# One-hots of a product-key expert layer: two tokens innermost, one compare instruction, chunks in pairs

## The chip, the cores and the metric

The kernel runs on one core of one Trainium2 chip. The metric is the device time of one execution in microseconds. TensorE (PE) multiplies matrices, VectorE (DVE) and ScalarE (ACT) do elementwise work, GpSimd (POOL) does next to nothing here, and SyncE (SP) issues the loads of weights. Every engine takes its own instructions in order.

## What is computed

The reference is a transformer of two blocks on 256 tokens of 1024 features in float32: two mixer layers with their feed-forwards, then attention, cross attention, and last a layer of 16,384 experts (PEER), which is the only part that the change touches:

```python
q = (xc @ w_q).reshape(PEER_TOK_CHUNK, PEER_HEADS, 2, half)
s = jnp.einsum("thpd,hpnd->thpn", q, subkeys)
s1, i1 = lax.top_k(s[:, :, 0], 16); s2, i2 = lax.top_k(s[:, :, 1], 16)
...                                   # the 16 best of the 16 x 16 sums, for each of 8 heads
e = jnp.take_along_axis(cand_i, top_pos, axis=-1)      # expert = 128 * i + j
g = jax.nn.softmax(top_s, axis=-1)
a = jax.nn.gelu(jnp.einsum("td,thkd->thk", xc, w_down[e]))
return jnp.einsum("thk,thkd->td", g * a, w_up[e])
```

So each token has 128 chosen experts (8 heads of 16), each with a weight g.

## The kernel before

The kernel doesn't gather. It multiplies all tokens with all 16,384 rows of `w_down`, keeps gelu of that in `act` [128 experts j, 128 chunks i, 256 tokens], multiplies it with a dense map of the weights g, which is zero for the experts that were not chosen, and multiplies the product with all of `w_up`.

**Chunks.** A chunk is 128 experts. `chunk` (line 1784) calls `lin_b`: `load` (line 223) fetches 512 KB of `pd`, ACT (L233) and DVE (L234) split it into a high and a low part (`wh`, `wl`, three buffers each), PE runs 24 matmuls of 256 columns (L257, L258, L260), and ACT takes the gelu out of PSUM. 70 chunks are done earlier, beside the routing. The other 58, the late chunks, are done between the groups of tokens described next.

**Weights of the chosen experts.** For each token the map [j, i] is a product of two one-hot matrices over the 128 slots: onehot(j) as the stationary operand, onehot(i) times g as the moving one. `iT` holds i, j and g of every slot with the slots on the partitions, `ib` holds them in float16 with g cut into a high part, and the low part stays in `iT`. A `group` (line 1849) does four tokens. Its `front` writes `oh` [128 slots, 4 kinds, 128, 4 tokens] in float16, with the four tokens innermost: DVE compares a table `rb` (0 to 127, each four times) with i, then with j (two instructions at L1854), and multiplies the first one-hot with the high part of g (L1855); ACT multiplies it with the low part, token by token (four at L1857). Its `back` runs two matmuls of 128 columns for each token (eight at L1865) into `pg`, DVE multiplies the activations of the chunks done so far with it in place (L1867), and ACT copies the rest of the map into the places of the chunks to come (L1869).

**Late chunks.** After each `back`, `upto` says how many chunks should be done by then, and `chunk(t0)` runs the missing ones. The tokens before t0 already have their weights in the chunk's place, so their gelu goes into a tile `ta` (L1792, three buffers), and DVE multiplies it in (L1796); the tokens from t0 on get their gelu directly (L1794). In the profile this is one late chunk for nearly every group.

**Order.** `pipe` runs the front of a group before the back of the group ahead of it. The tile framework then orders the instructions of each engine by priority and by its own estimates when it builds the program. `oh` has three buffers, `pg` four banks of PSUM. After the last group `lin_k` (line 341) multiplies `act` with `w_up` on PE, chunk by chunk, up to the end; `begin` starts its first three chunks a little earlier for the first 128 tokens.

Of the kernel before, what the change touches and what calls it, by code (L numbers as in the profile page):

```python
# [8 lines left out]
F32 = mybir.dt.float32  # L9
# [10 lines left out]
T = 256  # L20
# [5 lines left out]
# ---------------------------------------------------------------- host layout  # L26
# [4 lines left out]
def _pick(w, idx):  # L31
    """Columns idx of w; -1 stands for a column of zeros."""
    idx = np.asarray(idx)
    out = np.zeros((w.shape[0], len(idx)), w.dtype)
    ok = idx >= 0
    out[:, ok] = w[:, idx[ok]]
    return out


def _units(w, nk, ncol):  # L40
    """[K, N] -> units [n, 128, nk, ncol], k parts innermost among the units of a column block."""
    K, N = w.shape
    a = w.reshape(K // (128 * nk), nk, 128, N // ncol, ncol)
    return np.ascontiguousarray(a.transpose(3, 0, 2, 1, 4).reshape(-1, 128, nk, ncol))
# [6 lines left out]
def _pv(i):  # L51
    """Vectors that lie along the partitions: name -> [128, n]."""
# [28 lines left out]
def pack(i):  # L81
# [15 lines left out]
    # layer 0  # L97
# [20 lines left out]
    # layer 1  # L118
# [24 lines left out]
    # second block  # L143
# [17 lines left out]
    # constants of the shapes  # L161
# [24 lines left out]
# ---------------------------------------------------------------- kernel  # L186
def tile_kernel(tc, A, out, tap=None, stop=None):
# [7 lines left out]
    with contextlib.ExitStack() as ctx:  # L195
# [12 lines left out]
        def accs():  # L208
            """[token block][column half], tokens on partitions."""
            return [[f([128, 512], name="acc") for _ in range(2)] for f in (ps_lo, ps_at)]  # L210

        # ------------------------------------------------ helpers
# [5 lines left out]
        def pinned(*more, pins=True):  # L218
            """work of no hurry: after the instructions of the chain before it."""
            st = contextlib.ExitStack()  # L220
            for i in list(more) or (pools.pins if pins else []):
                st.enter_context(tc.issue_after(i))
            return st
# [17 lines left out]
        def ahead(*srcs):  # L241
            """fetch the weights of the next linears before what comes in between."""
# [11 lines left out]
        def mm3s(ps, pairs, start, stop):  # L254
            """the sum of mm3 over pairs (l, r), the products with the low part of r last."""
# [9 lines left out]
        def lin_b(src, u0, n, h, nk, kper, cper, evac, bank=None):  # L265
            """out^T chunks of 128 columns: units [128, kper, 128*cper], n units of columns."""
# [13 lines left out]
        def lin_n(src, h, evac):  # L280
            """as lin_b for one unit, in float32 passes without a split: where the vector engine holds the time."""
# [7 lines left out]
        def lin_a(src, u0, h, nk, kper, N, evac, between=None):  # L289
            """out [tok, N]: stationary h, moving the weights."""  # L290
# [13 lines left out]
        def split(dst, src, i=None):  # L304
            """dst pair (high, low) parts of src."""
# [13 lines left out]
        def mm_t(acc, a, w, tb, half, start, stop):  # L319
            """acc[tb][half] += a^T w: a [128, T], w [128, 2, 512]."""  # L320
# [7 lines left out]
        def tail(acc, parts, post, between=None):  # L328
            """the last parts (a, w), one token block after the other; post(acc, tb) when a block is complete;
            between: work before the second block's turn."""  # L330
# [12 lines left out]
        def lin_k(src, pool, chunks, post, turn, pre, keep=3, begun=None):  # L343
            """sum over chunks a of a^T W[k], tokens on partitions; post and turn: see tail.
            begun: the accumulators and the (a, w) of the first chunks, done for the first token block."""
# [20 lines left out]
        # ------------------------------------------------ constants  # L366
# [19 lines left out]
        # causal bias, [off block | diagonal block]  # L386
# [4 lines left out]
        def rms_steps(groups, n, out, eng=None):  # L391
            """1/rms over the features of each group of chunks, on all partitions: PSUM tiles [128, T] in out.
            groups: lists of (AP [128, w], w = T or 2T). Work for other engines fits between the steps."""
# [31 lines left out]
        def rsqrt(r, ss, scale):  # L425
            """r[:, 1] = (ss * scale + EPS) ** -0.5, r: [128, 4, ...] workspace."""
# [13 lines left out]
        def norm(src, out, n=1024, pin=False, between=None, eng=None):  # L440
            """out: [128, 1] = 1/rms of the rows of src, a list of APs [128, w]."""
# [29 lines left out]
        def rows(cols):  # L471
            """the vector cols [128, 8] along the free axis, on all partitions."""
# [10 lines left out]
        def postnorm(y, gr, tb, n, t):  # L483
            """x += gr * rmsnorm(y) for a token block, y: two PSUM halves; n: the next norm; t: [128, 2, 2, 512] workspace."""
# [26 lines left out]
        class raw:  # L511
            """the features of rmsnorm(x) * gain + shift before the division by the norm: pair h [128, 8, W],
            with the shift in columns T and T + 1 (an even number of them); r: 1/norm on all partitions, tok: with tokens on partitions."""
# [9 lines left out]
            def turn(self, tb, src=None, more=None):  # L523
                """a token block to features on partitions; more: (t, d), with diag(d) t to add to it."""
# [39 lines left out]
            def fin(self, pool, dst, ps, func=AF.Identity, scale=1.0):  # L564
                """dst = func(scale * (the linear of the normed features))."""
# [7 lines left out]
        # ------------------------------------------------ adaLN  # L573
# [24 lines left out]
        # ------------------------------------------------ attention of one head  # L598
        def pipe(jobs, lag=1):
            """jobs: (front, back) pairs; each back comes lag fronts after its own."""  # L600
# [10 lines left out]
        def attend(ap, q, k, v, o, bias, gate=None, full=False, first=True, last=True, rest=None):  # L611
            """q, k: [K, T]; v: two APs [128, dv]; o(): PSUM AP [dv, T], accumulated into unless first;
            gate: row factors [128, 2]. Returns the two parts of the work."""
# [47 lines left out]
        def after(job, f):  # L661
            """job with f() at its end."""
# [7 lines left out]
        class lazy:  # L670
            """a tile allocated at its first use."""
# [8 lines left out]
        # ================================================ layer 0 mixer  # L680
        def layer0():
            with contextlib.ExitStack() as ctx0:
# [25 lines left out]
                # the shift on the tensor engine, as a row  # L708
# [55 lines left out]
                def conv(c, ps):  # L764
                    """chunk c of the channels xs | B | C."""
# [20 lines left out]
                # dt and dt * a, tokens on partitions  # L786
# [23 lines left out]
                # strict lower (t > s) and upper (t <= l) masks, [t, .]  # L810
# [6 lines left out]
                # rope tables of the positions (cos | sin with the signs), the same on every 32 rows  # L817
# [28 lines left out]
                # S^T masked, [s, (blk0: l 0..255 | blk1: l 128..255)]  # L846
# [9 lines left out]
                # normed low rank parts of q and of k, v  # L856
# [12 lines left out]
                # xs * dt with tokens on partitions  # L869
# [167 lines left out]
        # ================================================ SwiGLU  # L1037
# [3 lines left out]
        def ffn(l):  # L1041
            with tpool(name=f"ffn{l}", bufs=2) as F:
# [56 lines left out]
                # keys and values of the memory, in the time of the norms  # L1099
# [35 lines left out]
        # ================================================ layer 1 mixer  # L1135
        def layer1():
            with contextlib.ExitStack() as ctx1:
# [22 lines left out]
                # ---- gated linear attention: cumulated log decay, [dk, t]  # L1160
# [15 lines left out]
                # gates with tokens on partitions: [128, qb, (head, branch)]  # L1176
# [21 lines left out]
                def evt(dst):  # L1198
                    """to tokens on partitions."""
# [11 lines left out]
                # ---- constants  # L1211
                # level masks [s, t]: t >= s and t xor s >= 2 ** level
                with pinned():
# [15 lines left out]
                    # bias of the heads: -slope * (q - k), masked; [off block | diagonal block]  # L1229
# [9 lines left out]
                    # the same for the compressed keys  # L1239
# [15 lines left out]
                # compressed keys and values  # L1255
# [3 lines left out]
                # [high | low] parts of the keys or values  # L1259
# [58 lines left out]
                def scores():  # L1318
                    """compressed scores: [128 q, qb, head, 32]"""
# [28 lines left out]
                # A^T [s, (head, blk0: t 0..255 | blk1: t 128..255)], level by level  # L1348
# [57 lines left out]
                def gla(hh):  # L1406
                    """with tokens on partitions."""
# [80 lines left out]
        # ================================================ MoBA + gMLP  # L1488
        def mix2():
            with contextlib.ExitStack() as ctx2:  # L1490
# [7 lines left out]
                # perm[k, m] = 1 where k = m ^ 32  # L1498
# [61 lines left out]
                # gMLP  # L1560
# [52 lines left out]
        class add_t:  # L1613
            """x += a^T W, units of 2 chunks and half of the columns; n: the next norm."""
# [5 lines left out]
            def go(self, tb, u):  # L1620
                """unit u for a token block."""
# [9 lines left out]
            def run(self, n, pre, first, last, post=None):  # L1631
                """first, last: units for both blocks together, for one after the other."""
# [16 lines left out]
        # ================================================ memory cross attention  # L1649
# [35 lines left out]
        # ================================================ PEER  # L1685
        def peer():
            with contextlib.ExitStack() as ctx4:
# [51 lines left out]
                def route(hh):  # L1739
                    """in steps, for other work in between; the last ones decode the chosen."""  # L1740
# [43 lines left out]
                def chunk(t0):  # L1784
                    """activations of 128 experts; the weights of the tokens before t0 stand in their place."""
# [3 lines left out]
                    def evac(_, ps):  # L1789
                        if t0:  # L1790
                            t = W4.tile([128, T], F32, name="ta", tag="ta", bufs=3)
                            S.activation(t[:, :t0], ps[:, :t0], AF.Gelu_apprx_tanh)  # L1792
                        if t0 < T:
                            S.activation(act[:, c, t0:], ps[:, t0:], AF.Gelu_apprx_tanh)  # L1794
                        if t0:
                            V.tensor_tensor(act[:, c, :t0], act[:, c, :t0], t[:, :t0], op=ALU.mult)  # L1796
# [14 lines left out]
                # softmax of the chosen scores (the first is the largest)  # L1811
# [20 lines left out]
                # 2 ** 15 times the weights in two parts of 11 bits and a sign: what a float32 holds  # L1832
                flat = sel.rearrange("p a b c -> p (a b c)").bitcast(F16)
                ib = flat[:, :1024].rearrange("p (e t) -> p e t", e=4)
                rb = flat[:, 1024:].rearrange("p (i t) -> p i t", t=4)
# [125 lines left out]
```

## Time and profile before

| | us |
|---|---|
| median of the timed runs | 1946.98 (1945.98 to 1949.31, 3 runs) |
| span of the profiled execution | 1948.3 |
| PE busy in it | 1911.8 (98%) |
| DVE busy | 1522.7 (78%) |
| ACT busy | 1129.0 (58%) |
| mean granted clock of TensorE | 0.993 |

Matmuls overlap in their pipeline, so a busy PE in the profile may still have room; how fast they follow one another is read from their starts. The stage that the change touches runs from 1357 to 1582 us, between the routing and the product with `w_up`.

### The profile page before, as it was taken

Reading aid. Unit: us, or ns where it says so; the run is one execution under the profiler, and the core shown is the slowest. Engines: PE = TensorE matmul, PEld = TensorE weight load, DVE = VectorE, ACT = ScalarE, POOL = GpSimd, SP = SyncE. Lnnn points to the kernel's source line nnn. Section 1 sums busy time; section 2 is a strip of 40 time slices with the busy share of each in tenths; the row PEclk is TensorE's granted clock in tenths of the full one; section 3 lists DMA queues with packets and bytes.
Section 4 is the critical chain, followed back from the end, with each engine's and each line's share of the span. In section 5 each row is a group of like instructions: output and inputs, shape, how many; then the busy total and the mean of one; then the engine's idle time right before and its main releaser. Section 6 shows DMA issues by size and latency. Waiting matters only on the chain.

```text
span 1948.3 us, 34549 instructions
## 1 busy us (share of the span) xinstructions
PE 1911.8 (98%) x12874; PEld 1714.4 (88%) x12874; DVE 1522.7 (78%) x3356; ACT 1129.0 (58%) x2170; POOL 12.9 (1%) x18
## 2 busy tenths in 40 slices
PE   7999999999999999999999999999999999999998
PEld 4988899999878899999988899999999988888886
DVE  7978889898778787677667798898899975555555
ACT  6876655467556555454655544445888854444444
POOL 0000000000000000000000000000000000000000
PEclk9999999999899999999999999999999999999999
DMA  9664698856316485545524455555444355555553
GB/s 331 220 205 151 203 325 276 278 193 206 122 66 229 163 312 181 176 152 178 184 92 147 133 179 180 195 181 174 149 135 141 131 185 192 186 189 190 184 191 133
DMA packets 102554, 362.12 MB, mean 186 GB/s; under 512 B 11617, under 2 KB 14689, under 8 KB 102130
## 3 DMA queue, kind: packets, MB, share of 16 engines
q1 hardware_dynamic: 100368, 357.61, 54.9%
q10 hardware_dynamic: 2018, 2.31, 0.4%
q8 instruction: 101, 1.65, 0.3%
q14 instruction: 67, 0.55, 0.1%
HBM read 357.25 MB, written 2.62 MB: 185 GB/s over the span
## 4 chain that ended last, share of the span: by engine, by line
PE 87%; DVE 7%; ACT 2%; DMA 1%; issue 1%; ACTq 0%; DVEq 0%
PE mm L257 11%; PE mm L260 11%; PE mm L258 11%; PE acc L252 10%; PE acc L250 10%; PE acc L251 10%; PE lo L257 3%; PE lo L260 3%; PE lo L258 3%; PE pg L1865 2%; DVE wl L234 2%; DVE act L1867 1%; PE sc L628 1%; PE pA L1354 1%; PE mm L250 1%
## 5 line engine op out<-in xcount | busy, mean ns | idle before, releaser
L234 DVE TENSOR_TENSOR wl<-w,wh 128x1024 fp32r<-128x1024 f32 (+1 forms) x571 | 694.7, 1220 | 159.7 <-ACT wh L233 154.2
L233 ACT ACTIVATE wh<-w 128x1024 fp32r<-128x1024 f32 (+1 forms) x571 | 598.5, 1054 | 244.3 <-PE mm L260 105.8
L257 PE MATMUL mm<-hh,wh 128*128 128x256 f32 (+1 forms) x2072 | 517.7, 287 | 4.5 <-DVE eb L569 1.4
L258 PE MATMUL mm<-hh,wl 128*128 128x256 f32 (+1 forms) x2072 | 511.9, 284 | 1.8 <-DVE wl L234 1.8
L257 PEld LDWEIGHTS mm<-hh,wh 128*128 128x128 f32 x2072 | 393.7, 190 | 9.5 <-issue 3.2
L258 PEld LDWEIGHTS mm<-hh,wl 128*128 128x128 f32 x2072 | 393.8, 190 | 4.7 <-DVE wl L234 2.5
L250 PE MATMUL acc<-wh,ah 128*128 128x512 f32 x784 | 310.7, 397 | 1.2 <-ACT ah L306 1.2
L252 PE MATMUL acc<-wh,al 128*128 128x512 f32 x784 | 309.4, 395 | 0.9 <-DVE al L307 0.9
L251 PE MATMUL acc<-wl,ah 128*128 128x512 f32 x784 | 309.6, 395 | 0.0
L260 PE MATMUL mm<-hl,wh 128*128 128x256 f32 (+1 forms) x2072 | 297.0, 283 | 0.0
L260 PEld LDWEIGHTS mm<-hl,wh 128*128 128x128 f32 x2072 | 267.9, 189 | 2.5 <-issue 2.0
L252 PEld LDWEIGHTS acc<-wh,al 128*128 128x128 f32 x784 | 147.4, 188 | 36.6 <-DVE al L307 1.3
L250 PEld LDWEIGHTS acc<-wh,ah 128*128 128x128 f32 x784 | 147.2, 188 | 35.6 <-ACT ah L306 2.2
L251 PEld LDWEIGHTS acc<-wl,ah 128*128 128x128 f32 x784 | 147.2, 188 | 33.9 <-DVE wl L234 0.3
L306 ACT ACTIVATE ah<-act 128x256 fp32r<-128x256 f32 (+1 forms) x131 | 53.7, 413 | 181.9 <-PE acc L251 177.5
L257 PE MATMUL lo<-hh,wh 128*128 128x256 f32 x520 | 128.7, 287 | 0.0
L258 PE MATMUL lo<-hh,wl 128*128 128x256 f32 x520 | 125.0, 279 | 0.0
L307 DVE TENSOR_TENSOR al<-act,ah 128x256 fp32r<-128x256 f32 (+1 forms) x131 | 54.4, 418 | 79.5 <-ACT ah L306 79.5
L586 DVE SCALAR_TENSOR_TENSOR wa<-wa,cbc 128x1024 f32<-128x1024 f32 x88 | 107.1, 1229 | 3.4 <-DMA wa<-in_ada 3.3
L1857 ACT ACTIVATE oh<-oh,iT 128x128 f16<-128x128 f16 x256 | 96.7, 572 | 4.7 <-DVE oh L1854 1.6
L257 PEld LDWEIGHTS lo<-hh,wh 128*128 128x128 f32 x520 | 98.2, 189 | 0.1
L258 PEld LDWEIGHTS lo<-hh,wl 128*128 128x128 f32 x520 | 97.9, 188 | 0.0
(567 smaller groups left out, 2448.0 us busy)
## 6 DMA issues: line engine op xcount, KB each, us to landing
w<-in_pd SPq DMA_DIRECT2D x128, 512.0 KB, 3.3
w<-in_pu SPq DMA_DIRECT2D x128, 512.0 KB, 3.2
wa<-in_ada SPq DMA_DIRECT2D x88, 512.0 KB, 4.5
w<-in_wf SPq DMA_DIRECT2D x88, 512.0 KB, 4.4
w<-in_w SPq DMA_DIRECT2D x79, 512.0 KB, 4.2
w<-in_wd SPq DMA_DIRECT2D x44, 512.0 KB, 4.1
w<-in_wo SPq DMA_DIRECT2D x32, 512.0 KB, 3.4
w<-in_pq SPq DMA_DIRECT2D x16, 512.0 KB, 3.7
```

The costliest lines, as they stand in the source:

```text
L233: S.activation(wh[:, :n], w[:, :n], AF.Copy)
L234: V.tensor_tensor(wl[:, :n], w[:, :n], wh[:, :n], op=ALU.subtract)
L250: PE.matmul(ps, lh[0], rh[0], start=start, stop=False, skip_group_check=True)
L251: PE.matmul(ps, lh[0], rh[1], start=False, stop=False, skip_group_check=True)
L252: PE.matmul(ps, lh[1], rh[0], start=False, stop=stop, skip_group_check=True)
L257: PE.matmul(ps, lh[0], rh[0], start=start and i == 0, stop=False, skip_group_check=True)
L258: PE.matmul(ps, lh[1], rh[0], start=False, stop=False, skip_group_check=True)
L260: PE.matmul(ps, lh[0], rh[1], start=False, stop=stop and i == len(pairs) - 1, skip_group_check=True)
L306: S.activation(dst[0], src, AF.Copy)
L307: return V.tensor_tensor(dst[1], src, dst[0], op=ALU.subtract).ins
L586: V.scalar_tensor_tensor(w, w, 1.0, pools.cbc, op0=ALU.mult, op1=ALU.mult, accum_out=mod[l][:, j:j + 1])
L1857: S.activation(oh[:, 3, :, t], oh[:, 0, :, t], AF.Copy, scale=iT[:, 2, t0 + t:t0 + t + 1])
```

## The change

`oh` becomes [128 slots, 4 kinds, 2 pairs of tokens, 128, 2 tokens]: two tokens are innermost, so the elements of one token's one-hot lie 4 bytes apart, where they lay 8 apart. `rb` holds each number twice, and `ib` is stored group by group, so that one instruction compares both i and j for all four tokens (1,024 elements for each slot) in the place of two of 512. The multiplication with the high part of g, the four of ACT and the eight matmuls stay, on the new layout. `upto` counts in twos, and late chunks come in pairs: two in a row after every second group or so. Their gelus go into the two halves of one tile `ta` (one buffer), and one instruction multiplies both in after the second.

```diff
-                def chunk(t0):
+                def chunk(t0, ta=None, last=True):
...
                         if t0:
-                            t = W4.tile([128, T], F32, name="ta", tag="ta", bufs=3)
-                            S.activation(t[:, :t0], ps[:, :t0], AF.Gelu_apprx_tanh)
+                            S.activation(ta[:, 1 if last else 0, :t0], ps[:, :t0], AF.Gelu_apprx_tanh)
                         if t0 < T:
                             S.activation(act[:, c, t0:], ps[:, t0:], AF.Gelu_apprx_tanh)
-                        if t0:
-                            V.tensor_tensor(act[:, c, :t0], act[:, c, :t0], t[:, :t0], op=ALU.mult)
+                        if t0 and last:
+                            V.tensor_tensor(act[:, c - 1:c + 1, :t0], act[:, c - 1:c + 1, :t0], ta[:, :, :t0],
+                                            op=ALU.mult)
...
-                ib = flat[:, :1024].rearrange("p (e t) -> p e t", e=4)
-                rb = flat[:, 1024:].rearrange("p (i t) -> p i t", t=4)
-                V.tensor_copy(rb, ri[:, :, None].to_broadcast([128, 128, 4]))
-                V.tensor_copy(ib[:, 0:2], iT[:, 0:2])
-                V.tensor_scalar(ib[:, 2], iT[:, 2], GS, None, op0=ALU.mult)
-                V.scalar_tensor_tensor(iT[:, 2], iT[:, 2], GS, ib[:, 2], op0=ALU.mult, op1=ALU.subtract)
+                ib = flat[:, :768].rearrange("p (g e q t) -> p g e q t", e=3, q=2, t=2)
+                rb = flat[:, 768:1024].rearrange("p (i t) -> p i t", t=2)
+                by4 = lambda e: iT[:, e].rearrange("p (g q t) -> p g q t", q=2, t=2)
+                V.tensor_copy(rb, ri[:, :, None].to_broadcast([128, 128, 2]))
+                for e in range(2):
+                    V.tensor_copy(ib[:, :, e], by4(e))
+                V.tensor_scalar(ib[:, :, 2], by4(2), GS, None, op0=ALU.mult)
+                V.scalar_tensor_tensor(by4(2), by4(2), GS, ib[:, :, 2], op0=ALU.mult, op1=ALU.subtract)
...
-                    return min(128, first + -(-(128 - first) * t // T) + 2)
+                    return min(128, first + 2 * -(-(128 - first) * t // (2 * T)) + 2)
...
-                        oh = W4.tile([128, 4, 128, 4], F16, name="oh", tag="oh", bufs=3)
-                        over = lambda t: t[:, None, t0:t0 + 4].to_broadcast([128, 128, 4])
-                        for e in range(2):
-                            V.tensor_tensor(oh[:, e], rb, over(ib[:, e]), op=ALU.is_equal)
-                        V.tensor_tensor(oh[:, 2], oh[:, 0], over(ib[:, 2]), op=ALU.mult)
+                        oh = W4.tile([128, 4, 2, 128, 2], F16, name="oh", tag="oh", bufs=3)
+                        of = ib[:, t0 // 4]
+                        V.tensor_tensor(oh[:, 0:2].rearrange("p e q i t -> p (e q) i t"),
+                                        rb[:, None].to_broadcast([128, 4, 128, 2]),
+                                        of[:, 0:2].rearrange("p e q t -> p (e q) t")[:, :, None]
+                                        .to_broadcast([128, 4, 128, 2]), op=ALU.is_equal)
+                        V.tensor_tensor(oh[:, 2], oh[:, 0], of[:, 2][:, :, None].to_broadcast([128, 2, 128, 2]),
+                                        op=ALU.mult)
                         for t in range(4):
-                            S.activation(oh[:, 3, :, t], oh[:, 0, :, t], AF.Copy, scale=iT[:, 2, t0 + t:t0 + t + 1])
+                            at = slice(t0 + t, t0 + t + 1)
+                            S.activation(oh[:, 3, t // 2, :, t % 2], oh[:, 0, t // 2, :, t % 2], AF.Copy,
+                                         scale=iT[:, 2, at])
...
-                                PE.matmul(p[:, t], oh[:, 1, :, t], oh[:, 2 + e, :, t], start=e == 0, stop=e == 1)
+                                PE.matmul(p[:, t], oh[:, 1, t // 2, :, t % 2], oh[:, 2 + e, t // 2, :, t % 2],
+                                          start=e == 0, stop=e == 1)
...
                         while done[0] < upto(t0 + 4):
-                            chunk(t0 + 4)
+                            ta = W4.tile([128, 2, T], F32, name="ta", tag="ta", bufs=1)
+                            chunk(t0 + 4, ta, last=False)
+                            chunk(t0 + 4, ta)
```

## Rows read from the trace of the kernel before

**Rows 1.** Busy time by stretch: start:end, length, then busy us and instructions by engine.

```profile
1357.00:1510.00 153.00, 152.96 (x1311) 150.83 (x1310) 140.62 (x259) 132.28 (x345) 0.00 (x0) 1.00 0.42 139
1510.00:1582.00 72.00, 69.92 (x585) 67.47 (x584) 71.80 (x118) 54.56 (x150) 0.00 (x0) 0.99 0.42 140
1357.00:1582.00 225.00, 222.87 (x1894) 218.29 (x1893) 212.42 (x376) 186.84 (x494) 0.00 (x0) 1.00 0.42 139
1582.00:1948.30 366.30, 357.83 (x1530) 286.14 (x1528) 215.44 (x280) 175.84 (x263) 2.49 (x2) 0.99 0.55 183
```

**Rows 2.** The chain that ended last, 1340 to 1600 us: start us, us, what.

```profile
1509.12 0.97 PE pg L1865 x8
1510.18 2.30 DVE act L1867 x2
1514.49 1.05 DVE wl L234
1515.88 1.14 DVE act L1867
```

**Rows 3.** Waits, 1357 to 1582 us: who waited for whom, us, times, longest us.

```profile
ACT act L1869 <- DVE act L1867: 31.1, 54, 1.0
DVE act L1867 <- PE pg L1865: 12.1, 31, 0.6
```

**Rows 4.** The same chain at its end, 1570 to 1625 us.

```profile
1578.73 1.29 DVE act L1867
1580.27 1.22 PE acc L252 x2
```

**Rows 5.** The chain between 1455 and 1475 us, one group and one chunk of PE.

```profile
1462.32 0.91 PE mm L260 x8
1463.22 0.95 PE pg L1865 x8
...
1466.00 0.91 PE lo L260 x8
1466.90 0.95 PE pg L1865 x8
```

**Rows 6.** Matmuls of 16-bit operands, by line: count, ns min/median/max, starts, shapes.

```profile
L1865 PE MATMUL pg<-oh x512: 277/297/330, 1357.9 to 1581.3; 128*128 128x128 f16 x171
L1865 PEld LDWEIGHTS <-oh x512: 111/117/147, 1357.7 to 1581.3; 128*128 128x128 f16 x171
L627 PEld LDWEIGHTS <-identb x32: 95/96/105, 114.9 to 1004.5; 128*128 128x128 bf16 x32
L627 PE MATMUL sc<-cb,identb x16: 221/226/230, 115.0 to 1004.5; 128*128 128x128 bf16 x16
L629 PE MATMUL sc<-cb,identb x16: 274/283/283, 115.5 to 1006.1; 128*128 128x256 bf16 x16
```

**Rows 7.** Order of time, 1530 to 1539 us, one group of DVE: start us, us, what.

```profile
1531.42 0.76 DVE L1854 TENSOR_TENSOR oh<-sel 128x512 f16<-128x512 f16 x2
1532.09 0.43 DVE L1855 TENSOR_TENSOR oh<-oh,sel 128x512 f16<-128x512 f16 x1
1532.42 1.23 DVE L234 TENSOR_TENSOR wl<-w,wh 128x1024 fp32r<-128x1024 f32 x1
1533.63 0.36 DVE L1796 TENSOR_TENSOR act<-act,ta 128x196 f32<-128x196 f32 x1
1533.91 1.27 DVE L1867 TENSOR_TENSOR act<-act,pg 128x468 f32<-128x468 f32 x1
```

**Rows 8.** DVE instructions by line: count, ns min/median/max, starts, shapes.

```profile
L1367 DVE TENSOR_TENSOR Eg<-bcum x8: 668/680/693, 495.5 to 570.3; 128x512 f32<-128x512 f32 x8
L1759 DVE TENSOR_TENSOR cand<-v x16: 403/411/421, 1123.8 to 1331.6; 128x256 f32<-128x256 f32 x16
L1777 DVE TENSOR_TENSOR cand<-cand,f x32: 402/414/420, 1133.6 to 1341.9; 128x256 f32<-128x256 f32 x32
L1796 DVE TENSOR_TENSOR act<-act,ta x58: 147/278/414, 1361.0 to 1577.1; 128x4 f32<-128x4 f32 x3, 128x8 f32<-128x8 f32 x1, 128x12 f32<-128x12 f32 x1, 128x16 f32<-128x16 f32 x1
```

More of the change, by code (lines that the diff above doesn't have):

```diff
@@ L1843, in peer @@
                 first = done[0]
+                assert first % 2 == 0
                 def upto(t):
-                    return min(128, first + -(-(128 - first) * t // T) + 2)
+                    return min(128, first + 2 * -(-(128 - first) * t // (2 * T)) + 2)
                 def group(t0):
                     def front():
-                        oh = W4.tile([128, 4, 128, 4], F16, name="oh", tag="oh", bufs=3)
-                        over = lambda t: t[:, None, t0:t0 + 4].to_broadcast([128, 128, 4])
-                        for e in range(2):
-                            V.tensor_tensor(oh[:, e], rb, over(ib[:, e]), op=ALU.is_equal)
-                        V.tensor_tensor(oh[:, 2], oh[:, 0], over(ib[:, 2]), op=ALU.mult)
+                        oh = W4.tile([128, 4, 2, 128, 2], F16, name="oh", tag="oh", bufs=3)
[6 more added lines that the diff above has]
+                                        op=ALU.mult)
```

## Prediction

> **What bounds the kernel now.** I first read the stretches and looked for the engine without idle time, then the chain that ended last, then the waits of the stage, and last the durations of single instructions. From 1357 to 1582 us the stage holds 222.9 us of PE work in 225 us; DVE has 212.4 and ACT 186.8 [rows 1]. The chain follows PE up to 1510 us and DVE from there on [rows 2]. Before 1510 DVE is idle for 153.0 - 140.6 = 12.4 us, and nearly all of that, 12.1 us, is L1867 waiting for the eight small matmuls of its group [rows 1, 3]; after 1510 DVE idles for 0.2 us. The two engines are thus nearly level: PE is a little dearer at first, and DVE catches up because L1867 and L1796 grow with the tokens. Time leaves this stage only if both become cheaper. What follows it is bound by PE (357.8 of 366.3 us), and its accumulation really starts when DVE has done the last groups [rows 1, 4], so what the stage gains, the kernel gains.
>
> **The change part by part.**
>
> **The eight matmuls (PE).** Eight take 0.95 us, 0.119 us each; a chunk takes from 1463.22 + 0.95 to 1466.90, 2.73 us [rows 5]. The 0.119 are twice too slow for their columns. Sixteen-bit operands whose elements lie side by side need 283 - 226 = 57 ns for 128 more columns, 0.45 ns a column [rows 6]; the 32-bit ones of the chunk, 4 bytes apart, need 0.91 / 8 / 256 = 0.44 ns [rows 5]; ours, 8 bytes apart, need 0.93, and one of ours lasts 297 ns where one of 128 columns side by side lasts 226, 71 ns more [rows 6]. Two and 4 bytes cost the same, 8 bytes twice as much. With two tokens innermost the step is 4 bytes, so I estimate 57 ns of columns. The weight load then counts too: it lasts 117 ns here and 96 ns side by side [rows 6], overlapped with other work, and the trace doesn't show how fast such loads can follow one another. Bounds: 57 ns at best, 119 ns for no gain, and not above, since no element comes to lie further apart. I take 64 ns, near the lower end, because the row of 4 bytes is the nearest. That is 8 x 64 x 0.055 = 28 us less PE work in the stage: 195 us.
>
> [...]
>
> **One compare for two (DVE).** One group of DVE reads, by starts: the two compares 0.67, the multiplication 0.33, the split of a chunk's weights 1.21, L1796 0.28, L1867 1.17 us to the next group's compare, 3.66 in all [rows 7]. The compares do two elements in a tick: 512 of float16 last as long (416 ns) as 256 of float32 [rows 7, 8]. At that rate 1,024 of them last as long as 512 of float32, 680 ns; back to back each instruction hides some 80 ns of its end under the next (416 against 335), so one compare takes 0.60 in the place of 0.67. That saves 0.067 x 64 = 4.3 us. The other end is one element a tick, 1.21 us as L234 takes for 1,024 [rows 7]; it is a rival below. I take the first, because the run of two tokens fills one 4-byte word, and one word read again and again costs nothing in the rows: L1759 repeats a single float32 word 16 times and lasts 411 ns, L1777 with no such repeat 414 [rows 8].
>
> **Pairs (DVE).** An L1796 of four elements lasts 147 ns, of which 67 aren't hidden [rows 8]; 29 of the 58 go, which saves 1.9 us. DVE falls from 212.4 to 206.2 us.
>
> **What stays.** ACT keeps all its instructions; for its copies at the new step I take the old price, since a change of either sign would hide in its 38 us of idle time. `upto` puts a chunk at most one earlier, so L1867 has on average two more elements, 0.1 us in the stage. The set-up before the first group gets one more small DVE instruction, under 0.4 us as its neighbours; PE runs a chunk meanwhile, and without that cover it would cost those 0.4 us once. Loads are the same 58 and move by one chunk at most on SP's queue.
>
> **The wait that pairs add.** PE runs 5.5 us of chunks without a small matmul between, and two groups' L1867 then wait for the pair's end and the two gelus. Behind a waiting L1867 on DVE stand the next compare and the next split, for which ACT and PE wait in turn. Three buffers of `oh` and three of split weights allow about one pair of work ahead. The single `ta` makes ACT hold the next pair's first gelu until the last multiplication is done, which comes some 3 us earlier. Below, each pair could cost nothing (DVE idles 0.2 us in the 72 us after 1510); above, 0.4 us, near the mean of the waits that L1867 has now (12.1 / 31) [rows 3]. I take 0.15 us for each of 29, 4.4 us, nearer to the lower end, since PE would have 11 us to spare.
>
> **The sum.** DVE 206.2 + 4.4 for hand-overs + 0.5 for the first groups, where four chunks instead of three stand at the start = 211 us for the stage in the place of 225: 14 us less. The profiled span of 1948.3 becomes 1934; the median of the runs was 1.3 us below the span, so 1933 us. If no hand-over costs anything and DVE sheds another microsecond, 1927; at 0.4 us each pair, 1940, and with ACT late by the same it may be 1942.
>
> **The rivals.**
> - **PE stays.** The small matmuls keep 0.119 us, because their pace is set by something other than the step, the weight load say (117 ns long, which speaks for it; that 226 ns rows exist speaks against). PE stays at 222.9 and only the last 72 us gain the 0.1 us per group of DVE: 1945 us.
> - **The waits move.** In-order engines with pairs wait for one another as long as DVE waits now. For it: ACT already spends 31.1 us of its idle time behind L1867 [rows 3], and 186.8 + 31.1 = 218 us would leave 7 of 225; pairs make the bursts longer. Against: those waits are slack while PE or DVE is the bound. With 218 to 224 us for the stage: 1940 to 1946, say 1944 us.
> - **DVE loses its two per tick.** If a run of two tokens isn't enough for it, the compare takes 1.21 in the place of 0.67, and the multiplication (512 elements) 0.60 in the place of 0.33: 0.81 us for each of 64 groups, 52 us. DVE has 212.4 - 1.9 + 52 = 262 us, and the stage with it: 1984 us. It decides from the point at which the group grows by more than the idle 12.4 us hide, 0.2 us. Against it is the repeated word of L1759.
>
> [...]
>
> **How the numbers follow.** Forecast 0.66 (own range 1927 to 1942). PE stays 0.09; the waits move 0.12; DVE loses its rate, whole or in part (1955 to 1984), 0.13. A difference of 0.2%, 3.9 us, is about what a measurement of this kernel can tell from no change. Faster: the forecast and a third of the moved waits, 0.70. Same: 0.09 and the rest of the moved waits without a small loss, 0.16. Slower: 0.14. The range is 1926 to 1949: it holds the forecast and the two rivals that end near no change, 0.85 or so, and leaves out the slow DVE.
>
> **What would show it.** L1865 at about 230 ns each and eight in 0.5 us; one compare of 1,024 at 680 ns and the multiplication still at 416; 29 of L1796; L1867's wait for `pg` near nothing; DVE without idle time in a stage of some 211 us. A compare of 1.2 us, eight small matmuls still in 0.95 us, or new waits of L1867 or ACT of over 0.4 us for each pair would make the prediction wrong.

## The result, and the profile after

| | before | after |
|---|---|---|
| median of the timed runs, us | 1946.48 | 1958.06 (1956.53 to 1959.11) |
| ratio to before, 95% interval | | 1.0056 [1.0039, 1.0072] |
| span of the profiled execution, us | 1948.3 | 1954.8 |

The kernel became slower by 0.6%, where 0.7% faster was forecast. In the changed kernel the merged compare is L1859, the multiplication L1863, ACT's copies L1867, the small matmuls L1876, the multiplication of the activations L1879 (L1867 before) and ACT's copy of the map L1881 (L1869 before). The splits stay L233 (ACT) and L234 (DVE).

I read the durations first. By line, of the whole execution: count, ns min/median/max, starts, shapes.

```profile
L1876 PE MATMUL pg<-oh x512: 217/218/330, 1355.2 to 1587.3; 128*128 128x128 f16 x171
L1876 PEld LDWEIGHTS <-oh x512: 96/97/147, 1355.1 to 1587.2; 128*128 128x128 f16 x171
L1859 DVE TENSOR_TENSOR oh<-sel x64: 668/686/716, 1353.8 to 1583.4; 128x1024 f16<-128x1024 f16 x64
L1863 DVE TENSOR_TENSOR oh<-oh,sel x64: 403/420/450, 1354.7 to 1585.2; 128x512 f16<-128x512 f16 x64
L1867 ACT ACTIVATE oh<-oh,iT x256: 403/431/452, 1354.8 to 1585.1; 128x128 f16<-128x128 f16 x128
```

Every instruction that the change touches is about as cheap as forecast: the small matmul 218 ns in the place of 297 [rows 6], the compare of 1,024 elements 686 ns (680 forecast), the multiplication 420 (416). So the loss is not in the work. The stretches show where it is: start:end, length, then busy us and instructions of PE, PEld, DVE, ACT and POOL, the granted clock, DMA.

```profile
1357.00:1510.00 153.00, 143.75 (x1312) 138.67 (x1311) 129.18 (x187) 120.41 (x331) 0.00 (x0) 0.98 0.42 139
1510.00:1582.00 72.00, 62.87 (x548) 59.09 (x548) 65.03 (x84) 51.53 (x154) 0.00 (x0) 0.95 0.38 126
1357.00:1590.00 233.00, 210.99 (x1876) 201.13 (x1876) 201.46 (x282) 173.97 (x490) 0.00 (x0) 0.96 0.41 135
1590.00:1954.80 364.80, 356.34 (x1525) 286.43 (x1524) 213.71 (x277) 175.30 (x260) 2.49 (x2) 0.99 0.55 182
```

The stage ends near 1590 us where it ended at 1582 [rows 1]. It also begins earlier in this profile, with the first compare at 1353.8 us in the place of 1356.4; from the first compare to the end of the last L1879 it takes 235.2 us, and by the same measure 226.6 before. Before, PE had no idle time up to 1510 and DVE none from there on; now no engine is full anywhere. PE is idle for 22 of 233 us, DVE for 233.0 - 201.5 = 31.5. What follows the stage takes 364.8 us where it took 366.3 [rows 1], so nothing is lost there. DVE's busy time of 201.5, or 204.0 if one counts from 1353.8 to 1589 us, lies under the 206.2 that I had summed. The waits of 1357 to 1592 us name what DVE's idle time is (who waited for whom: us in all, times, longest):

```profile
ACT act L1881 <- DVE act L1879: 36.5, 42, 1.7
DVE wl L234 <- ACT wh L233: 24.6, 18, 1.6
...
PE pg L1876 <- DVE oh L1863: 10.7, 9, 4.6
ACT oh L1867 <- DVE oh L1859: 10.1, 21, 3.0
...
DVE act L1796 <- ACT ta L1792: 5.2, 5, 1.4
```

Of the 31.5 us, 24.6 are the split L234 waiting for ACT's half of it, L233, in 18 waits over 29 pairs; the stage didn't have this wait before. 5.2 are the pair's multiplication waiting for a gelu. The wait that I wanted to remove, the activations' multiplication waiting for `pg` (12.1 us in L1867 before [rows 3]), is down to 0.4 us. Two engines' queues in order of time show how the new one comes about (start us, us, what, idle time before it and its releaser). DVE:

```profile
1463.07 1.23 DVE L234 TENSOR_TENSOR wl<-w,wh 128x1024 fp32r<-128x1024 f32 x1 [1.39 <-ACT wh L233]
1464.21 0.39 DVE L1796 TENSOR_TENSOR act<-act,ta 128x232 f32<-128x232 f32 x1
1464.52 2.09 DVE L1879 TENSOR_TENSOR act<-act,pg 128x400 f32<-128x400 f32 x2
1466.52 1.28 DVE L1859 TENSOR_TENSOR oh<-sel 128x1024 f16<-128x1024 f16 x2
1467.73 0.75 DVE L1863 TENSOR_TENSOR oh<-oh,sel 128x512 f16<-128x512 f16 x2
1468.40 1.21 DVE L234 TENSOR_TENSOR wl<-w,wh 128x1024 fp32r<-128x1024 f32 x1
1470.99 1.23 DVE L234 TENSOR_TENSOR wl<-w,wh 128x1024 fp32r<-128x1024 f32 x1 [1.38 <-ACT wh L233]
```

And ACT in the same microseconds:

```profile
1466.65 0.38 ACT L1881 ACTIVATE act<-pg 128x112 f32<-128x112 f32 x1 [0.63 <-DVE act L1879]
1467.23 1.62 ACT L1867 ACTIVATE oh<-oh,iT 128x128 f16<-128x128 f16 x5 [0.21 <-DVE oh L1859]
1468.72 0.25 ACT L1792 ACTIVATE ta<-mm 128x124 f32<-128x124 f32 x1
1468.87 0.26 ACT L1794 ACTIVATE act<-mm 128x132 f32<-128x132 f32 x1
1469.03 1.02 ACT L1867 ACTIVATE oh<-oh,iT 128x128 f16<-128x128 f16 x3
1469.91 1.05 ACT L233 ACTIVATE wh<-w 128x1024 fp32r<-128x1024 f32 x1
```

Pairs of chunks make pairs of everything. DVE does two L1879 in a row, two compares, two multiplications and two splits. ACT idles until the first L1879 and the first compare let it go (1467.23), and then has eight copies and two gelus before the L233 that DVE's second split needs. DVE is through with its own work at 1469.6 and waits for 1.38 us. Then it splits, multiplies the pair and runs the L1879 for which ACT waits: each waits for the other in turn. From one such L234 to the next are 7.92 us. The parts of this loop add up to that: on DVE L234, L1796 and two L1879 up to 1466.52 (3.45), the first compare up to 1467.23 (0.71), on ACT copies and gelus up to 1469.91 (2.68), L233 up to DVE's next start (1.08). The trace's chain of work that ended last comes from PE into this round, at 1464.2 us, and then goes the same way, from DVE to ACT and back:

```profile
1461.28 0.94 PE pg L1876 x16
...
1464.60 2.01 DVE act L1879 x2
1466.61 0.60 DVE oh L1859
1467.23 0.70 ACT oh L1867 x3
...
1470.05 0.92 ACT wh L233
1470.99 0.19 DVE wl L234
```

### The profile page after: what moved, and what is told of

Its sections match the earlier page's. It is cut to its first block, busy times and chain, and to the rows that moved or that the text cites. A ratio compares the mean times of both kernels' runs of the same rounds, so it can differ in the third digit from the quotient of the medians.

```text
span 1954.8 us, 34309 instructions
## 1 busy us (share of the span) xinstructions
PE 1898.5 (97%) x12874; PEld 1698.0 (87%) x12874; DVE 1512.2 (77%) x3264; ACT 1118.4 (57%) x2169; POOL 13.0 (1%) x18
## 4 chain that ended last, share of the span: by engine, by line
PE 81%; DVE 10%; ACT 5%; issue 2%; DMA 2%; ACTq 0%; DVEq 0%; SPq 0%
PE mm L257 10%; PE mm L260 10%; PE mm L258 10%; PE acc L252 10%; PE acc L250 10%; PE acc L251 10%; PE lo L258 3%; PE lo L257 2%; PE lo L260 2%; DVE act L1879 2%; DVE wl L234 2%; ACT oh L1867 2%; ACT wh L233 1%; DMA wa<-in_ada 1%; PE sc L628 1%
## 5 line engine op out<-in xcount | busy, mean ns | idle before, releaser
L234 DVE TENSOR_TENSOR wl<-w,wh 128x1024 fp32r<-128x1024 f32 (+1 forms) x571 | 694.8, 1220 | 185.6 <-ACT wh L233 179.8
L233 ACT ACTIVATE wh<-w 128x1024 fp32r<-128x1024 f32 (+1 forms) x571 | 598.7, 1054 | 245.8 <-PE mm L260 103.5
L257 PE MATMUL mm<-hh,wh 128*128 128x256 f32 (+1 forms) x2072 | 521.1, 288 | 3.9 <-DVE eb L569 1.4
L258 PE MATMUL mm<-hh,wl 128*128 128x256 f32 (+1 forms) x2072 | 516.0, 285 | 5.5 <-DVE wl L234 5.5
L258 PEld LDWEIGHTS mm<-hh,wl 128*128 128x128 f32 x2072 | 395.1, 191 | 9.9 <-DVE wl L234 7.7
L257 PEld LDWEIGHTS mm<-hh,wh 128*128 128x128 f32 x2072 | 394.5, 190 | 9.7 <-issue 3.2
L258 PE MATMUL lo<-hh,wl 128*128 128x256 f32 x520 | 128.8, 285 | 5.1 <-DVE wl L234 5.1
L257 PE MATMUL lo<-hh,wh 128*128 128x256 f32 x520 | 129.7, 286 | 0.0
L258 PEld LDWEIGHTS lo<-hh,wl 128*128 128x128 f32 x520 | 99.6, 191 | 5.9 <-DVE wl L234 5.9
L257 PEld LDWEIGHTS lo<-hh,wh 128*128 128x128 f32 x520 | 99.4, 191 | 0.0
L1867 ACT ACTIVATE oh<-oh,iT 128x128 f16<-128x128 f16 x256 | 85.8, 432 | 12.7 <-DVE oh L1859 10.1
```

Of the source, the lines that this page charges most:

```text
L233: S.activation(wh[:, :n], w[:, :n], AF.Copy)
L234: V.tensor_tensor(wl[:, :n], w[:, :n], wh[:, :n], op=ALU.subtract)
L257: PE.matmul(ps, lh[0], rh[0], start=start and i == 0, stop=False, skip_group_check=True)
L258: PE.matmul(ps, lh[1], rh[0], start=False, stop=False, skip_group_check=True)
L1867: S.activation(oh[:, 3, t // 2, :, t % 2], oh[:, 0, t // 2, :, t % 2], AF.Copy, scale=iT[:, 2, at])
```

## The experiments

Times are medians; ratios are to the kernel before, on the same chip, with 95% intervals.

**One part at a time.** `e1_single` keeps all but the pairs:

```diff
-                            ta = W4.tile([128, 2, T], F32, name="ta", tag="ta", bufs=1)
-                            chunk(t0 + 4, ta, last=False)
-                            chunk(t0 + 4, ta)
+                            chunk(t0 + 4)              # own ta of three buffers, own L1796, upto in ones
```

> The new layout and the one compare, with late chunks one at a time as before (three ta buffers, one L1796 for each chunk). If the pairs of chunks are what costs, the waits between engines go and the work of DVE (about 204 us in the stage) sets its length: 1930 to 1937 us. If the new layout or the single compare is what makes the engines wait, the time stays above 1950 us.

`e2_pairs` is the kernel before with pairs alone:

```diff
+                            ta = W4.tile([128, 2, T], F32, name="ta", tag="ta", bufs=1)
+                            chunk(t0 + 4, ta, last=False)
+                            chunk(t0 + 4, ta)
-                            chunk(t0 + 4)
```

> The kernel before with pairs alone: four tokens innermost, two compares, late chunks two at a time. If the pairs cost, it is slower than the kernel before by the same waits, on top of small matmuls that still take 0.119 us each: 1960 to 1975 us. If they don't: 1943 to 1947 us.

`e3_layout` is `e1_single` with two compares again, so the new layout alone:

```diff
-                        V.tensor_tensor(oh[:, 0:2]..., is_equal)      # [128, 4, 128, 2]
+                        for e in range(2):
+                            V.tensor_tensor(oh[:, e], rb..., of[:, e]..., op=ALU.is_equal)   # [128, 2, 128, 2]
```

> The new layout alone: two tokens innermost, two compares of 512 elements, chunks one at a time. If the compare's merging is worth what its duration says (0.067 us for each of 64 groups), this is 3 to 5 us above the run with the one compare; if PE alone bounded the stage, the two are equal. With pairs as the cause of the loss: 1933 to 1941 us; with the layout as the cause: above 1950 us.

| | us | ratio |
|---|---|---|
| `e1_single`: layout and compare | 1938.34 | 0.9941 [0.9924, 0.9958] |
| `e2_pairs`: pairs | 1961.87 | 1.0065 [1.0048, 1.0081] |
| `e3_layout`: layout | 1936.03 | 0.9935 [0.9918, 0.9951] |

The pairs are the loss: on the old layout 1961.87 - 1949.33 = 12.5 us, on the new one 1.0056 - 0.9941 = 0.0115 of 1946.5, 22 us (19.7 by the medians, which are from chips on which the kernel before took 1946.5 and 1949.3; so I go by ratios). On the old layout they cost less: there DVE had idled 12.1 us behind the small matmuls [rows 3], in `e2_pairs` that wait is 2.1 us (up to 1570 us), and so part of the new wait only stands in the old one's place. The layout alone gains some 13 us, about what was forecast for the whole change. A gain from the compare isn't shown: the intervals of `e1_single` and `e3_layout` lie over each other, and `e3_layout`, expected 3 to 5 us above, came out 2.3 below. A wait of each, 1357 to 1566 us, shows one difference. First `e1_single`, where ACT's copies (here L1865) wait for the one compare (L1857):

```profile
ACT oh L1865 <- DVE oh L1857: 13.4, 43, 0.5
```

and then `e3_layout`, where the first of the two compares (L1858) is enough to let the copies (L1864) go:

```profile
ACT oh L1864 <- DVE oh L1858: 1.3, 7, 0.2
```

The compare itself is cheaper as forecast: all 64 of `e1_single` are busy for 43.5 us, the 128 of `e3_layout` for 47.8. But from the first compare to the end of the last multiplication with `pg`, DVE's busy time as a whole is the same, 210.1 and 210.3 us, and DVE is idle for 6.8 us in `e1_single` and 1.4 in `e3_layout`. Whether ACT's later start brings this about isn't shown: the order of DVE's queue differs too (in `e1_single` a split stands between compare and multiplication near 1462 and 1471 us).

The stage of `e3_layout` is what the forecast described. Measured like that it runs from 1352.4 to 1564.1 us, 211.7 us long, and from 1357 to 1560 us DVE is full (201.67 of 203):

```profile
1357.00:1560.00 203.00, 196.97 (x1854) 191.88 (x1853) 201.67 (x362) 174.21 (x483) 0.00 (x0) 0.99 0.46 152
```

Its DVE queue shows no wait, and ACT's next to it shows why. One group of each (here L1876 multiplies the activations, L1860 the one-hots):

```profile
1463.09 0.74 DVE L1858 TENSOR_TENSOR oh<-sel 128x512 f16<-128x512 f16 x2
1463.76 0.41 DVE L1860 TENSOR_TENSOR oh<-oh,sel 128x512 f16<-128x512 f16 x1
1464.10 1.21 DVE L234 TENSOR_TENSOR wl<-w,wh 128x1024 fp32r<-128x1024 f32 x1
1465.23 0.28 DVE L1795 TENSOR_TENSOR act<-act,ta 128x136 f32<-128x136 f32 x1
1465.44 1.11 DVE L1876 TENSOR_TENSOR act<-act,pg 128x412 f32<-128x412 f32 x1
1466.48 0.74 DVE L1858 TENSOR_TENSOR oh<-sel 128x512 f16<-128x512 f16 x2
...
1467.48 1.20 DVE L234 TENSOR_TENSOR wl<-w,wh 128x1024 fp32r<-128x1024 f32 x1
```

```profile
1463.59 1.32 ACT L1864 ACTIVATE oh<-oh,iT 128x128 f16<-128x128 f16 x4
...
1465.10 1.05 ACT L233 ACTIVATE wh<-w 128x1024 fp32r<-128x1024 f32 x1
```

Here four copies stand ahead of L233, which ends at 1466.15, and DVE comes to that split at 1467.48: 1.3 us to spare, where the pairs leave it 1.4 us short. A group takes 3.39 us from compare to compare, two of them 6.8; the pairs take 7.9 for the same work.

**Is it the multiplication that the two share?** `e7_unshared` runs two chunks in a row as the change does, but gives each its own `ta` and its own L1796:

```diff
-                            ta = W4.tile([128, 2, T], F32, name="ta", tag="ta", bufs=1)
-                            chunk(t0 + 4, ta, last=False)
-                            chunk(t0 + 4, ta)
+                            chunk(t0 + 4)              # own ta of three buffers, own L1796
+                            chunk(t0 + 4)
```

> The changed kernel with two late chunks in a row as it has, but each multiplied in by its own instruction, with three ta buffers. If it is the shared multiplication, which waits for the second gelu, or its single tile, the loss of the pairs goes: 1938 to 1942 us. If it is the two chunks in a row, the time stays where the changed kernel is, plus up to 2 us for 29 more instructions: 1957 to 1963 us.

1955.26 us, 1.0039 [1.0025, 1.0054]: a little under the expected 1957, and the interval overlaps that of the changed kernel. At most a few of the 22 us can be due to the shared instruction or the single buffer of `ta`. The wait of L234 stays (up to 1570 us), and `e2_pairs` has it on the old layout, 26.0 us in 22 times. In `e7_unshared`:

```profile
DVE wl L234 <- ACT wh L233: 24.0, 20, 1.6
```

It comes with two chunks in a row, on either layout and with either way to multiply them in.

**Are ACT's copies part of it?** `e6_nolow` takes them out of the changed kernel, and `e8_single_nolow` takes them out of `e1_single`. Both leave out the low part of the weights g; the second matmul of each token stays and uses the high part again, so PE's work is the same:

```diff
-                        for t in range(4):
-                            S.activation(oh[:, 3, ...], oh[:, 0, ...], AF.Copy, scale=iT[:, 2, at])
...
-                                PE.matmul(p[:, t], oh[:, 1, ...], oh[:, 2 + e, ...], start=e == 0, stop=e == 1)
+                                PE.matmul(p[:, t], oh[:, 1, ...], oh[:, 2, ...], start=e == 0, stop=e == 1)
```

> The changed kernel without ACT's copies at L1867: the low part of the weights is left out, and both matmuls of a token use the high part, so PE's work stays. Theory: with pairs, ACT has eight copies (2.6 us) in its queue ahead of the split of the next weights, DVE waits for that split, and ACT waits for DVE's next compares; without the copies this loop is shorter than DVE's own work: 1932 to 1942 us, within 5 us of the next run. If the loss comes from PE's or DVE's own order, it stays above 1950 us.

> The same cut (no low part, no copies of ACT) with chunks one at a time: the reference for the run before it. DVE's work bounds it: 1932 to 1938 us under either theory, since the run with copies and single chunks gave 1938 us with little waiting for ACT.

1930.09 us, 0.9908 [0.9892, 0.9925], with pairs and 1931.61 us, 0.9919 [0.9902, 0.9935], without them. Both are a little under the expected 1932 us. Without the copies, pairs cost nothing that can be told. `e6_nolow`, 1357 to 1560 us, has DVE at 198.5 of 203 us, and L234's wait is 0.7 us in that stretch:

```profile
1357.00:1560.00 203.00, 196.25 (x1886) 192.83 (x1884) 198.50 (x277) 101.23 (x237) 0.00 (x0) 1.00 0.46 152
```

ACT has 73 us less work here, and yet it was far from full with the copies too (174 of 233 us). That speaks for their place in the queue as the cost, and not their sum; the next two runs put it to the test.

**Is it the order in ACT's queue?** If so, putting the splits of the next pair ahead of the copies must give time back with all work in place. `e5_ahead` does it for the first chunk of the next pair, `e9_ahead2` for both:

```diff
                             chunk(t0 + 4, ta)
+                            if done[0] < 128:
+                                ahead(A["pd"][done[0]])                           # e5_ahead
+                                ahead(A["pd"][done[0]], A["pd"][done[0] + 1])     # e9_ahead2, in its place
```

> The changed kernel, pairs kept, but the first weights of the next pair are asked for right behind the pair, ahead of the next fronts in the program. If the place of that split in ACT's queue is what makes DVE wait, part of the loss goes: 1940 to 1952 us. If not: 1956 to 1960 us.

> The changed kernel, with the split of both chunks of the next pair put right behind the present pair, where the run before put only the first of them there (1947.8 us). Theory, order in ACT's queue (the second split stands behind the copies of two groups, so DVE and ACT wait for each other in turn): most of the second split now stands ahead of copies, DVE's waits for it fall from 8.5 us in the stage to under 5, and the time goes on from 1947.8 towards the 1938.3 of single chunks: 1939 to 1944 us. Rival, what is left are the other hand-overs of a pair (the two gelus behind two groups' copies, copies waiting for the longer compare), which do not depend on where the splits stand: 1946 to 1950 us. Second rival, the three buffers of split weights make the second early split wait for PE with copies queued behind it: slower than 1950 us.

`ahead` moves a chunk's whole load up: its DMA, ACT's L233 and DVE's L234. The DMA is hardly what counts, since in the changed kernel L233 waits for it for 1.0 us in the whole stage; the places in ACT's and in DVE's queue weren't moved one without the other.

1947.84 us, 1.0006 [0.9996, 1.0016], and 1942.6 us, 0.9965 [0.9954, 0.9976]. Of the 22 us that pairs cost, the first split's place gives back 0.0050, 10 us, and the second's another 0.0041, 8 us. The wait of L234, in `e5_ahead` (up to 1576 us) and in `e9_ahead2` (up to 1566 us):

```profile
DVE wl L234 <- ACT wh L233: 10.0, 7, 2.6
```

```profile
DVE wl L234 <- ACT wh L233: 6.4, 9, 1.4
```

Over the same stretch (up to 1566 us) the wait falls from 8.5 to 6.4 us, where under 5 was expected; the time came out as expected. So the place of the splits in the two queues is shown to be most of the cause. What still parts `e9_ahead2` from single chunks (0.9941) is 0.0024, 5 us, and the two intervals just overlap. Beside it stand 5.6 us in which L1796 waits for a gelu and the 6.4 us above; these weren't taken apart.

**A faster kernel.** `e3_layout` beats both kernels. Two edits on top of it were tried, because its stage ends with waits of PE, 3.3 and 1.3 us, for the first operands of the next one: `f1_begin` starts the first chunks of the product with `w_up` earlier, `f2_ahead` sets the split of the next chunk behind the present one, and `f3_both` has both.

```diff
-                for j, at in reversed(list(enumerate((64, 64, 64)))):
+                for j, at in reversed(list(enumerate((62, 63, 64)))):            # f1_begin, f3_both
...
                             chunk(t0 + 4)
+                            if done[0] < 128:
+                                ahead(A["pd"][done[0]])                          # f2_ahead, f3_both
```

> Two tokens innermost, two compares, chunks one at a time, and the first three chunks of the last product started between the last groups instead of behind them. In the run without this last edit PE stood idle for 4.5 us at the end of the stage, since those chunks' splits waited for the last L1867. If that wait goes: 1930 to 1934 us, 2 to 6 us below that run. If DVE, which has to do the same work, holds the end anyway: 1935 to 1938 us.

> Two tokens innermost, two compares, chunks one at a time, and the weights of the next chunk asked for right behind each chunk, as in the run that did this for pairs. With single chunks DVE waits 0 to 7 us in the stage, so little is to be had: 1932 to 1937 us. If the place of the split in ACT's queue costs here too, 1930 us; if the early split delays the compares on DVE, 1938 to 1942 us.

> The new layout with two compares and single chunks, with both small edits together: the first chunks of the next stage begin two and one groups earlier, and the next chunk's split stands right behind the present chunk. Alone they gave 1933.7 and 1934.0 us where 1936.0 was without them, within each other's intervals. If both gains are real and lie in different places (the end of the stage, and its middle), 1931 to 1932 us; if they are the same few waits, or no gain at all, 1933 to 1936 us.

1933.73 us (0.9922 [0.9900, 0.9944]), 1934.02 (0.9927 [0.9905, 0.9948]) and 1934.83 (0.9930 [0.9908, 0.9952]). All intervals overlap that of `e3_layout`, so neither edit is shown to help. In `f1_begin` PE still waits for 5.0 us for the first operands of the next stage (1540 to 1580 us): the wait that the edit aimed at didn't go. What is shown is 0.65% for the layout with single chunks.

## Why the prediction was wrong

**The wait that pairs add** is the step that failed. I took 0.15 us for each pair and 0.4 as its upper bound. Measured, with all else equal: 22 us / 29 = 0.77 us. That is 18 us more than the 4.4 us in the sum, of the 25 us that lie between 1933 and 1958. The rest is about the 4.3 us of the compare, which didn't arrive, and the 1.9 us of the 29 saved L1796, which can't be seen. The stage grew by 8.6 us where I had it shrink by 14, and the time lies 9 us above the range's upper end. Three things in that step were wrong.
- The bound came from the mean of L1867's waits for `pg` [rows 3], another wait with another cause. A sum along the loop would have been the one to make, and its terms were there: two L1867, compares, eight copies (567 ns each in the kernel before), a split on each engine.
- "Three buffers of `oh` and three of split weights allow about one pair of work ahead" told what the buffers allow. It didn't tell what the order in the queues lets through, and there the second L233 stood behind the copies of two groups. `e5_ahead` and `e9_ahead2` have the same buffers and other places of the splits, and got back 18 of 22 us.
- I named ACT's idle time as its reserve (38 us before, 59 now). ACT was idle for a quarter of the stage and still late in most rounds: 36.5 and 10.1 us of its idle time stood behind L1879 and the compare. The 31.1 us of [rows 3] were a sign of this, and I called them slack.

**The rival "the waits move"** had the mechanism, and named ACT, but was priced at 1944 us, because I let the waits grow to what DVE's old ones were. **"DVE loses its two per tick"** held most of my chance for a slower kernel, and it didn't happen: the compare lasts 686 ns, where the whole loss was priced at 1.2 us. No run shows the 1955 us of a loss in part; 686 ns, and 420 for the multiplication, show none.

**The eight matmuls**: right. The forecast was 64 ns each. Sixteen take 0.94 us in the chain of the changed kernel at 1461.28 us, 59 ns each. Their busy time is 40.8 us over the stage of `e3_layout` and was 70.5, so the 28 us of the forecast are there. PE's busy time as a whole fell less, from 224.5 to 204.4 us, where I had 195; part of that stretch runs at a lower granted clock (0.97 from 1510 to 1560 us), and the rest wasn't taken apart. One small matmul lasts 297 ns with elements 8 bytes apart [rows 6] and 218 with 4.

**One compare for two**: its duration was right (686 for 680 ns) and its gain wrong. The compares take 4.3 us less, as forecast, but DVE's busy time as a whole is the same with one compare and with two, and DVE is idle for 5.4 us more. ACT's wait for the longer instruction, 13.4 us where two compares leave 1.3, stands beside this; that it is the cause isn't shown. Compare and multiplication took 686 and 420 ns, where 512 elements of float32 take 680 [rows 8] and the multiplication took 416 before: a run of one word, read again and again, keeps the rate here.

**Pairs** in themselves: 29 instructions of L1796 as counted, and a saving too small to see (`e7_unshared`, with all 58, isn't slower).

**What stays**: "ACT keeps the old price" was wrong to the good side, 431 in the place of 567 ns. The copies stand in the loop, but back to back the gain there is small: eight copies and two gelus take 2.87 us in a round of `e2_pairs` (1463.47 to 1466.34 us), with the old step, and 2.68 in the round shown above.

**The rest of the sum** was nearly right. Without the pairs' two terms (4.4 and 1.9 us) it gives some 1930 us for the layout with one compare, and some 1935 with two. By their ratios, from 1946.5 us, `e1_single` is at 1935.0 and `e3_layout` at 1933.8: the layout was priced within 2 us, and the compare's gain is what is missing.

## What to carry to other kernels

Before grouping work that passes between two engines, write down both queues for one round and add up the path from an engine back to itself: a group of two doubled what stood ahead of the last hand-over here, and neither free buffers nor idle time in the sum protected against that. An engine at 75% (ACT, 174 of 233 us) can be the one that is late; moving the instruction that others wait for ahead in the queues gave back 18 of 22 us with all work in place. Merging two instructions takes from the next engine the early half on which to start: here the 64 merged compares took 43.5 us and the 128 of `e3_layout` 47.8, but ACT's copies waited for 13.4 us where two compares leave 1.3, and no gain was left to be seen.

## What the runs showed of the hardware

**ACT's copies go by the step too.** A copy of 128 float16 elements took 567 ns (median) with elements 8 bytes apart and takes 431 with 4 bytes, with the same count and type. The copies of the kernel before:

```profile
L1857 ACT ACTIVATE oh<-oh,iT x256: 547/567/602, 1357.2 to 1576.3; 128x128 f16<-128x128 f16 x128
```

**TensorE's granted clock fell in the middle of the stage.** In the kernel before the granted clock is 1.00 from 1357 to 1510 us [rows 1]. In the changed kernel PE has gaps, 22 of 233 us, and in four stretches of 3.41 us between 1440 and 1564 us the granted clock is 0.50. A stretch ahead of the first of them, this one, and the next:

```profile
1430.00:1440.50 10.50, 8.84 (x74) 7.65 (x74) 9.12 (x14) 8.32 (x25) 0.00 (x0) 1.00 0.29 100
1440.55:1443.96 3.41, 3.41 (x19) 3.41 (x17) 2.45 (x5) 3.12 (x9) 0.00 (x0) 0.50 0.40 154
1484.92:1488.33 3.41, 3.41 (x17) 3.41 (x18) 3.36 (x5) 1.87 (x5) 0.00 (x0) 0.50 0.57 178
```

PE was idle for 1.7 us of the 10.5 ahead of the first fall. At 0.50 it is busy throughout, with 19 matmuls in the records of the first such stretch: L257 and L258 start 0.21 us apart there (1440.55 to 1443.10 us), and 0.12 us apart at 1.00 (1434.01 to 1435.78 us). This is likely part of why PE shows 211 us of busy time in the changed kernel. What it added to the time wasn't measured by itself, and falls don't come with pairs alone: `e3_layout`, with single chunks, shows 0.97 from 1510 to 1560 us.
